# Attention heads taken in pairs: score products of two heads side by side, value products alternating

## The chip, the cores and the metric

The kernel runs on one core of a Trainium2 chip. Its engines are TensorE (PE in the profile, with PEld for its weight loads), VectorE (DVE), ScalarE (ACT), GpSimd (POOL) and SyncE (SP, which issues the transfers). The metric is the device time of one execution in microseconds (us), lower is better; the time before is the median of three runs.

## The reference

Two transformer blocks over 256 tokens of width 1024, all in float32. The first block has two layers; each has 12 self-attention heads and 4 heads over a memory of 256 rows, all of width 64, and a gated feed-forward net. The second block has 8 attention heads of width 96 (values of width 64) beside a recurrent branch, and then a layer of 16384 experts.

```python
# first block, layer 0: forgetting attention (layer 1: causal with ALiBi)
s = q @ k.T * scale + F[t] - F[s]          # causal
out = softmax(s) @ v                       # 12 heads of width 64
mem_out = softmax(qm @ mk.T * scale) @ mv  # 4 heads of width 64, 256 keys
# second block
s = where(mask, q @ k.T * scale, min)      # 8 heads, q and k of width 96
out = softmax(s) @ v                       # v of width 64
```

## The kernel before, in words

Weights stream from DRAM in blocks of 128x1024, 512 KB each. ACT makes a high part `hi` of every block (line L201) and DVE, or for some blocks POOL, the rest `lo` (L203); every projection is then three products per chunk (L238 to L240). A projection of one block is 24 matmuls of 128x256. A block is split two blocks ahead of its use, through three buffers for `lo`.

Attention works with one head at a time. `scores` makes, for the two token tiles, a negated score product on PE (L364); in a self head the first tile has 128 keys and the second 256, in a memory head both have 256. Heads of width 64 use 64 of the array's 128 rows: head 0 of a pair the lower half of the partitions, head 1 the upper half. In layer 0 a second product (L366, 128 rows) adds the forgetting terms at once. DVE adds the mask and takes the row minimum (L369, L373), ACT takes the exponential (L374), DVE scales the rows by their inverse sums (L379, L381): the result is `P`. `values` transposes `P` on PE (L396), copies the transposes to `PT` (ACT at L403 and DVE at L405 in turn), and multiplies by the values (L406, and L408 or L410). Its output has 64 columns of the array: head 0 writes partitions 0 to 63 of a PSUM tile, head 1 partitions 64 to 127. These products have float32 operands, and the trace has two matmuls for each.

`layer` queues the `values` calls: while the scores of pair c are made, the two heads of pair c - 1 wait, and two projections of the next pair's keys and queries lie between. In `mixers` (second block) a head's `values` come after the two `mg` projections of the next head.

The order of instructions on each engine is not that of the code: the framework's scheduler sets it when the program is built, by its own estimate of times. An engine then runs its list in order, and waits on semaphores where a result isn't there.

The tiles that the prediction names: `pa` and `pb` are PSUM tiles (four buffers each), `kT`, `qT`, `mkT`, `qmT`, `QT` keys and queries, `SA` and `MB` the forgetting terms, `V`, `MV`, `KV` values, `xth`/`xtl` and `h1h`/`h1l` the two parts of a projection's input, `hdh`, `at` the heads' output, `rr`, `ii`, `xc` the recurrent branch (scans at L1228, products on POOL at L1227).

Of the kernel before, what the change touches and what calls it, by code (L numbers as in the profile page):

```python
# [8 lines left out]
F32 = mybir.dt.float32  # L9
# [14 lines left out]
#: Buffers of the weight stream, and how many blocks ahead of their use the blocks are split.  # L24
# [16 lines left out]
#: The blocks from which on the row factors of the two norms are there, and the first query block of whole h2.  # L41
# [3 lines left out]
#: The blocks whose low parts gpsimd computes, and the channels that it convolves.  # L45
# [4 lines left out]
#: Expert chunks ahead of the first gates; chunks in the first expert buffer; chunks of the tail.  # L50
# [91 lines left out]
def expert_order():  # L142
    """What the tensor engine does in the expert layer: u chunks, groups of gates, v chunks."""
# [10 lines left out]
class Stream:  # L154
    """Weight blocks from DRAM, each split exactly into two float32r parts (high + low)."""
# [9 lines left out]
    def on_pool(self, key):  # L165
        """Where the vector engine has much else to do, gpsimd takes a part of the subtractions."""
# [52 lines left out]
class Net:  # L219
# [28 lines left out]
    def setup(self):  # L248
# [23 lines left out]
        # the clock of the tensor engine rises with use: have it up when the input arrives  # L272
# [111 lines left out]
    def values(self, state, v, po):  # L384
# [7 lines left out]
        for kb in range(2):  # L392
            for tt in range(2):
                if causal and kb > tt:
                    continue
# [1171 lines left out]
```

## Time and profile before

| what | before |
|---|---|
| time, median of 3 runs | 1764.59 us (1763.13 to 1770.04) |
| profiled execution, first to last instruction | 1766.2 us |
| PE busy in it | 1713.1 us, 97% |
| PEld, DVE, ACT, POOL busy | 1563.5, 1242.2, 888.9, 412.1 us |

The profile records the span of its execution and nothing around it, so 1766.2 us is the profiled execution's own time here; it lies 1.6 us above the median. Matmuls overlap in the pipeline: what one costs is read from the distance between starts, not from its duration. A row of the timeline merges what follows each other: its first number is the start, the second the time from the first start to the last end, and the text names the first of them. A number in square brackets is the idle time ahead of it.

### The profile page before, as it was taken

What the parts mean: (1) busy time and instruction counts of PE and PEld (TensorE: products, weight loads), DVE (VectorE), ACT (ScalarE), POOL (GpSimd) and SP (SyncE); (2) the same over time, 40 slices, a digit from 0 to 9 for tenths busy, and PEclk for the clock granted to TensorE, in tenths of its full rate; (3) what the DMA queues carried; (4) which work ended last, traced back from release to release, by engine and by line L of the source; (5) the groups of instructions that cost most, each with busy time, mean ns of one, the idle gap of its engine ahead of it and who ended that gap; (6) DMA issues with size and microseconds to landing.
All of it is one profiled execution on the core that took longest, in us unless ns stands there. A gap on an engine that the chain in (4) does not pass through costs nothing.

```text
span 1766.2 us, 30939 instructions
## 1 busy us (share of the span) xinstructions
PE 1713.1 (97%) x11722; PEld 1563.5 (89%) x11722; DVE 1242.2 (70%) x2417; ACT 888.9 (50%) x1502; POOL 412.1 (23%) x463
## 2 busy tenths in 40 slices
PE   8999999999999999888999999999999999999998
PEld 7779989888899998777999989999999988888887
DVE  6656767766577768886775968977888755555555
ACT  7444544464454446587654444444444444444443
POOL 5100000001000004344032324278888300000000
PEclk9999999999999999989999999999999999999999
DMA  6324777753377765433456555454444556665663
GB/s 218 119 96 162 251 235 252 255 181 108 111 251 253 254 225 165 137 120 117 158 168 203 172 166 165 156 168 138 138 143 143 179 189 186 189 188 190 190 188 123
DMA packets 86803, 311.44 MB, mean 176 GB/s; under 512 B 9728, under 2 KB 11008, under 8 KB 86144
## 3 DMA queue, kind: packets, MB, share of 16 engines
q1 hardware_dynamic: 86480, 308.43, 53.6%
q8 instruction: 92, 1.51, 0.3%
q10 hardware_dynamic: 144, 1.05, 0.2%
q14 instruction: 55, 0.45, 0.1%
q0 software_dynamic: 32, 0.00, 0.0%
HBM read 307.35 MB, written 2.10 MB: 175 GB/s over the span
## 4 chain that ended last, share of the span: by engine, by line
PE 69%; DVE 16%; DMA 7%; issue 3%; ACT 2%; POOL 1%; SPq 0%; DVEq 0%; ACTq 0%; POOLq 0%
PE pb L240 10%; PE pb L239 10%; PE pa L238 10%; PE pb L238 10%; PE pa L239 10%; PE pa L240 10%; DMA raw<-in_w_ada_dram 6%; DVE lo L203 5%; PE pa L1430 3%; PE pa L364 2%; PE pb L406 1%; ACT hi L201 1%; DMA raw<-in_w_gate_dram 1%; PE pb L396 1%; DVE gu L645 1%
## 5 line engine op out<-in xcount | busy, mean ns | idle before, releaser
L203 DVE TENSOR_TENSOR lo<-raw,hi 128x1024 fp32r<-128x1024 f32 (+3 forms) x498 | 620.5, 1248 | 315.3 <-issue 202.7
L201 ACT ACTIVATE hi<-raw 128x1024 fp32r<-128x1024 f32 (+1 forms) x532 | 555.6, 1046 | 447.3 <-PE pb L239 227.9
L240 PE MATMUL pb<-h1h,lo 128*128 128x256 f32 x1264 | 361.6, 286 | 10.5 <-DVE lo L203 8.9
L238 PE MATMUL pb<-h1h,hi 128*128 128x256 f32 x1264 | 367.4, 291 | 0.8 <-ACT gl L1002 0.8
L239 PE MATMUL pb<-h1l,hi 128*128 128x256 f32 x1264 | 360.8, 285 | 0.0
L240 PE MATMUL pb<-xth,lo 128*128 128x256 f32 (+1 forms) x936 | 266.3, 285 | 3.1 <-DVE lo L203 3.0
L238 PE MATMUL pb<-xth,hi 128*128 128x256 f32 (+1 forms) x936 | 266.1, 285 | 0.0
L239 PE MATMUL pb<-xtl,hi 128*128 128x256 f32 (+1 forms) x936 | 265.3, 284 | 0.0
L240 PEld LDWEIGHTS pb<-h1h,lo 128*128 128x128 f32 x1264 | 242.3, 192 | 13.0 <-DVE lo L203 10.9
L238 PEld LDWEIGHTS pb<-h1h,hi 128*128 128x128 f32 x1264 | 242.5, 192 | 1.7 <-ACT gl L1002 1.0
L239 PEld LDWEIGHTS pb<-h1l,hi 128*128 128x128 f32 x1264 | 242.3, 192 | 0.7 <-issue 0.5
L1429 POOL TENSOR_SCALAR ring<-iota,slots 128x128 f32<-128x128 f32 x256 | 210.2, 835 | 42.4 <-PE pa L1430 42.0
L238 PE MATMUL pa<-hi,ring_v 128*128 128x512 f32 x512 | 202.1, 395 | 0.0
L240 PE MATMUL pa<-hi,ring_v 128*128 128x512 f32 x512 | 202.0, 395 | 0.0
L239 PE MATMUL pa<-lo,ring_v 128*128 128x512 f32 x512 | 202.0, 395 | 0.0
L240 PEld LDWEIGHTS pb<-xth,lo 128*128 128x128 f32 (+1 forms) x936 | 176.9, 189 | 6.4 <-DVE lo L203 4.2
L239 PEld LDWEIGHTS pb<-xtl,hi 128*128 128x128 f32 (+1 forms) x936 | 177.1, 189 | 2.9 <-issue 0.9
L238 PEld LDWEIGHTS pb<-xth,hi 128*128 128x128 f32 (+1 forms) x936 | 176.9, 189 | 2.3 <-issue 0.3
L203 POOL TENSOR_TENSOR lo<-raw,hi 128x1024 fp32r<-128x1024 f32 x34 | 91.4, 2688 | 180.4 <-PE pb L240 117.3
L240 PEld LDWEIGHTS pa<-hi,ring_v 128*128 128x128 f32 x512 | 96.5, 188 | 22.5
L238 PEld LDWEIGHTS pa<-hi,ring_v 128*128 128x128 f32 x512 | 96.5, 188 | 22.5
L239 PEld LDWEIGHTS pa<-lo,ring_v 128*128 128x128 f32 x512 | 96.5, 188 | 22.3
(427 smaller groups left out, 2795.0 us busy)
## 6 DMA issues: line engine op xcount, KB each, us to landing
raw<-in_expert_u_dram SPq DMA_DIRECT2D x128, 512.0 KB, 3.6
raw<-in_expert_v_dram SPq DMA_DIRECT2D x128, 512.0 KB, 4.3
raw<-in_w_ada_dram SPq DMA_DIRECT2D x48, 512.0 KB, 4.5
raw<-in_w_gate_dram SPq DMA_DIRECT2D x44, 512.0 KB, 4.2
raw<-in_w_up_dram SPq DMA_DIRECT2D x44, 512.0 KB, 4.4
raw<-in_w_down_dram SPq DMA_DIRECT2D x44, 512.0 KB, 4.4
raw<-in_w_out_dram SPq DMA_DIRECT2D x24, 512.0 KB, 3.6
raw<-in_w_mg_dram SPq DMA_DIRECT2D x16, 512.0 KB, 3.2
```

Of the source, the lines that this page charges most:

```text
L201: first = nc.scalar.activation(hi[:, :w], raw[:, :w], AF.Copy)
L203: self.last = first, eng.tensor_tensor(lo[:, :w], raw[:, :w], hi[:, :w], OP.subtract)
L238: mm(out, s[0], m[0], start=start, stop=False)
L239: mm(out, s[0], m[1], start=False, stop=False)
L240: mm(out, s[1], m[0], start=False, stop=stop)
L364: nc.tensor.matmul(p[:, :nk], qT[:, ts], kT[:, :nk], start=True, stop=extra is None)
L396: nc.tensor.transpose(pt[:, off:off + 128], P[:, R[tt][0] + kb * 128:R[tt][0] + (kb + 1) * 128], self.ident)
L406: nc.tensor.matmul(po, v(0), PT[:, 0:T], start=True, stop=False, skip_group_check=True)
L645: nc.vector.tensor_tensor(gu, p.rearrange("p (a t) -> p a t", a=2), rb[:, None, :].to_broadcast([128, 2, T]), OP.mult)
L1429: nc.gpsimd.tensor_scalar(ob, iota, slots[:, 1, t:t + 1], None, op0=OP.is_equal)
L1430: nc.tensor.matmul(p[:, j * 128:(j + 1) * 128], oa, ob, start=True, stop=True, skip_group_check=True)
```

## The change

`scores` takes one head or two. With two it makes the products of both heads next to each other (tile 0 of both, then tile 1 of both), all in four PSUM tiles, and only then the four products with the forgetting terms; the exponentials and the scaling follow for both heads. `values` takes a pair: the six (memory: eight) transposes of both heads, a copy of the first head's to `PT` on ACT and of the second's on DVE, then the value products of the two heads in turn, by blocks of 128 keys. In the second block, where q and k have 96 rows, scores are still made for one head at a time, and the values of a pair come together, after the projections that follow its second head. Lines of comment are taken out elsewhere, so line numbers differ.

```diff
-    def scores(self, qT, kT, causal, bias, extra=None):
-        nc = self.nc
-        P, R = self.att.tile([128, 384 if causal else 512], F32, tag="P", name="P"), []
...
+    def scores(self, qk, causal, bias, extra=None):
+
+        nc, n = self.nc, len(qk)
+        ps = []
         for tt in range(2):
             nk = 128 * (tt + 1) if causal else T
             ts = slice(tt * 128, (tt + 1) * 128)
-            p = self.psA()
-            nc.tensor.matmul(p[:, :nk], qT[:, ts], kT[:, :nk], start=True, stop=extra is None)
-            if extra is not None:
-                nc.tensor.matmul(p[:, :nk], extra[0][:, ts], extra[1][:, :nk], start=False, stop=True)
...
+            ps.append([self.psA()[:, :nk] for _ in range(n)])
+            for (qT, kT), p in zip(qk, ps[tt]):
+                nc.tensor.matmul(p, qT[:, ts], kT[:, :nk], start=True, stop=extra is None)
+        if extra is not None:
+            for tt in range(2):
+                for (sel, rows), p in zip(extra, ps[tt]):
+                    nc.tensor.matmul(p, sel[:, tt * 128:(tt + 1) * 128], rows[:, :p.shape[1]], start=False, stop=True)
...
+    def values(self, states, v, po):
+
+        nc = self.nc
+        causal = states[0][1][0][1] == 128
+        PTs = []
+        for s, (P, R) in enumerate(states):
+            pt = self.psB()
+            off = 0
+            for kb in range(2):
+                for tt in range(2):
+                    if causal and kb > tt:
+                        continue
+                    nc.tensor.transpose(pt[:, off:off + 128], P[:, R[tt][0] + kb * 128:R[tt][0] + (kb + 1) * 128],
+                                        self.ident)
+                    off += 128
+            PT = self.att.tile([128, 512], F32, tag="PT", name="PT")
+            if s == 0:
+                nc.scalar.copy(PT[:, :off], pt[:, :off])
             else:
-                s = p
...
+                nc.vector.tensor_copy(PT[:, :off], pt[:, :off])
+            PTs.append(PT)
         for kb in range(2):
...
+            for s, PT in enumerate(PTs):
+                o = po[s * 64:(s + 1) * 64]
+                if kb and causal:
+                    nc.tensor.matmul(o[:, 128:T], v(s, 1), PT[:, T:T + 128], start=False, stop=True,
+                                     skip_group_check=True)
+                else:
+                    nc.tensor.matmul(o, v(s, kb), PT[:, kb * T:(kb + 1) * T], start=kb == 0, stop=kb == 1,
+                                     skip_group_check=True)
...
-            states = []
-            for s in range(2):
-                rows = slice(s * 64, (s + 1) * 64)
-                states.append(self.scores(qmT[rows, b, :], mkT[rows, b, :], False, None))
+            halves = [slice(s * 64, (s + 1) * 64) for s in range(2)]
+            states = self.scores([(qmT[rows, b, :], mkT[rows, b, :]) for rows in halves], False, None)
...
-            finish(1)
-            waiting.append(head_values(h, self.scores(QT[0][:, h, :], QT[1][:, h, :], True, cm)))
+            if h % 2 == 0:
+                finish(0)
+            states += self.scores([(QT[0][:, h, :], QT[1][:, h, :])], True, [cm])
+            if h % 2:
+                waiting.append(pair_values(h - 1, states))
+                states = []
```

The built order of SP and POOL is the same in both programs. That of PE, DVE and ACT differs in three stretches alone: from the first memory scores to the output projection in each of the two layers, and from the `mg` projections to the second block's output projections. Two places show it.

The first is PE in layer 0, between two projections of keys and queries: the scores of one pair (L364, in the changed program L365; `SA` terms at L366, then L369) and the transposes and values of the pair before (L396, L406, L408, then L410, L426, L423). Before:

```order
L364 MATMUL pa<-kT,qT 128x128
L366 MATMUL pa<-MB,SA 128x128
L364 MATMUL pa<-kT,qT 128x256
L366 MATMUL pa<-MB,SA 128x256
L396 MATMUL pb<-ident,P 128x128 x3
L364 MATMUL pa<-kT,qT 128x128
L366 MATMUL pa<-MB,SA 128x128
L364 MATMUL pa<-kT,qT 128x256
L406 MATMUL pb<-PT,V 64x256
L408 MATMUL pb<-PT,V 64x128
L396 MATMUL pb<-ident,P 128x128 x3
```

In the changed program, at the best ordered of the six pairs:

```order
L365 MATMUL pa<-kT,qT 128x256 x2
L369 MATMUL pa<-MB,SA 128x128 x2
L369 MATMUL pa<-MB,SA 128x256 x2
L410 MATMUL pb<-ident,P 128x128 x6
L365 MATMUL pa<-kT,qT 128x128 x2
L365 MATMUL pa<-kT,qT 128x256
L426 MATMUL pb<-PT,V 64x256 x2
L423 MATMUL pb<-PT,V 64x128 x2
```

The products with 64 rows, with 128 rows and with 64 columns, which took turns one by one, now stand in groups. In the other pairs the scheduler has put some of them elsewhere: one score product of a pair alone, or two to nine projection matmuls between the first value product of head 0 and that of head 1. The memory scores stand as four in a row in both programs.

The second place is the first pair of the second block, on PE: before, the transposes of its first head (`P_8754`), the scores of two later heads, the first head's values, and then 48 projection matmuls ahead of the second head's transposes.

```order
L396 MATMUL pb_8929<-ident_94,P_8754 128x128 x3
L364 MATMUL pa_8940<-QT1_8260,QT0_8259 128x128
L364 MATMUL pa_8945<-QT1_8260,QT0_8259 128x256
L364 MATMUL pa_9037<-QT1_8260,QT0_8259 128x128
L364 MATMUL pa_9042<-QT1_8260,QT0_8259 128x256
L406 MATMUL pb_8928<-PT_8933,KV_8230 64x256
L408 MATMUL pb_8928<-PT_8933,KV_8230 64x128
```

In the changed program the second head's transposes (`P_8845`) follow at once, the values of both heads stand together, and the 48 matmuls come behind them, with 48 more ahead of the next pair's transposes:

```order
L410 MATMUL pb_8929<-ident_94,P_8758 128x128 x3
L410 MATMUL pb_8935<-ident_94,P_8845 128x128 x3
L365 MATMUL pa_8947<-QT1_8260,QT0_8259 128x128
L365 MATMUL pa_8949<-QT1_8260,QT0_8259 128x256
L365 MATMUL pa_9034<-QT1_8260,QT0_8259 128x128
L365 MATMUL pa_9036<-QT1_8260,QT0_8259 128x256
L426 MATMUL pb_8928<-PT_8933,KV_8230 64x256
L426 MATMUL pb_8928<-PT_8939,KV_8230 64x256
L423 MATMUL pb_8928<-PT_8933,KV_8230 64x128
L423 MATMUL pb_8928<-PT_8939,KV_8230 64x128
```

DVE at the same place, in the changed program: the scans of the recurrence, the scaling of the second head's `P_8845`, the `lo` parts of two weight blocks, and then the copy `PT_8939` that the second head's values need. Before, the same rows stand there without the copy.

```order
L1237 SCALAR_TENSOR_TENSOR rr_8257<-rr_8257,ii_8258 128x256 x4
L393 RECIPROCAL inv_8854<-sums_8846 128x2
L395 TENSOR_SCALAR P_8845<-P_8845,inv_8854 128x128
L395 TENSOR_SCALAR P_8845<-P_8845,inv_8854 128x256
L203 TENSOR_TENSOR lo_8897<-raw_8726,hi_8896 128x1024
L203 TENSOR_TENSOR lo_8971<-raw_8781,hi_8970 128x1024
L417 COPY PT_8939<-pb_8935 128x384
```

So PE reaches the need for `P_8845` and `PT_8939` 48 matmuls sooner, while DVE's list ahead of them is as long as before.

## Rows read from the trace of the kernel before

**Rows 1.** The page: its span and the busy time of the engines.
```profile
span 1766.2 us, 30939 instructions
PE 1713.1 (97%) x11722; PEld 1563.5 (89%) x11722; DVE 1242.2 (70%) x2417; ACT 888.9 (50%) x1502; POOL 412.1 (23%) x463
```

**Rows 2.** Busy time by stretch: layer 0, layer 1, second block.
```profile
core 0: us, PE busy (x) PEld busy (x) DVE busy (x) ACT busy (x) POOL busy (x), PEclk, DMA share, GB/s
50.00:144.00 94.00, 91.94 (x601) 75.12 (x602) 54.02 (x153) 40.53 (x99) 0.00 (x0) 0.98 0.29 96
394.00:476.00 82.00, 81.55 (x580) 67.53 (x577) 52.17 (x151) 39.88 (x97) 8.54 (x10) 1.00 0.31 102
776.00:856.00 80.00, 73.79 (x532) 68.34 (x533) 51.79 (x104) 62.94 (x116) 28.12 (x27) 0.92 0.34 119
```

**Rows 3.** PE's longest waits in layer 0 (first row) and in layer 1.
```profile
PE pa L364 <- DVE qmT L588: 1.7, 1, 1.7
...
PE pb L406 <- ACT PT L403: 0.2, 1, 0.2
```

**Rows 4.** Timeline of PE, layer 0: scores and values of one pair.
```profile
101.14 0.48 PE L364 MATMUL pa<-kT,qT 64*128 64x128 f32 x2
101.55 0.33 PE L366 MATMUL pa<-MB,SA 128*128 128x128 f32 x1
101.81 0.70 PE L364 MATMUL pa<-kT,qT 64*128 64x256 f32 x2
102.44 0.39 PE L366 MATMUL pa<-MB,SA 128*128 128x256 f32 x1
102.67 0.49 PE L396 MATMUL pb<-ident,P 128*128 128x128 f32 x3
...
104.39 0.65 PE L406 MATMUL pb<-PT,V 128*64 128x256 f32 x2
104.87 0.38 PE L408 MATMUL pb<-PT,V 128*64 128x128 f32 x2
105.18 0.55 PE L396 MATMUL pb<-ident,P 128*128 128x128 f32 x3
```

**Rows 5.** Timeline of PE, layer 0: projections, memory scores of one pair, projection.
```profile
53.40 0.28 PE L238 MATMUL pb<-xth,hi 128*128 128x256 f32 x1
53.52 0.28 PE L239 MATMUL pb<-xtl,hi 128*128 128x256 f32 x1
53.73 1.14 PE L364 MATMUL pa<-mkT,qmT 64*128 64x256 f32 x8
54.80 0.38 PE L240 MATMUL pb<-xth,lo 128*128 128x256 f32 x1
```

**Rows 6.** Timeline of PE, layer 1: scores of two heads in a row, of one head.
```profile
409.95 0.93 PE L364 MATMUL pa<-kT,qT 64*128 64x128 f32 x8
...
413.16 0.92 PE L364 MATMUL pa<-kT,qT 64*128 64x128 f32 x4
414.01 0.65 PE L406 MATMUL pb<-PT,MV 128*64 128x256 f32 x2
```

**Rows 7.** Timeline of PE, second block: scores, then values of two heads.
```profile
798.11 1.48 PE L364 MATMUL pa<-QT,QT 96*128 96x128 f32 x8
800.07 0.65 PE L406 MATMUL pb<-PT,KV 128*64 128x256 f32 x2 [0.48 <-ACT PT L403]
...
813.59 1.11 PE L406 MATMUL pb<-PT,KV 128*64 128x256 f32 x2 [5.61 <-DVE PT L405]
```

**Rows 8.** Timeline of DVE over the same stretch.
```profile
800.20 1.27 DVE L381 TENSOR_SCALAR P<-P,inv 128x128 f32<-128x128 f32 x2
801.40 3.44 DVE L203 TENSOR_TENSOR lo<-raw,hi 128x1024 fp32r<-128x1024 f32 x2
...
813.00 0.53 DVE L405 COPY PT<-pb 128x384 f32<-128x384 f32 x1
```

**Rows 9.** Busy time and granted clock behind the long wait (columns as in group 2).
```profile
813.60:818.90 5.30, 5.30 (x22) 4.58 (x23) 0.81 (x3) 2.94 (x4) 0.00 (x0) 0.50 0.35 137
```

More of the change, by code (lines that the diff above doesn't have):

```diff
@@ L374, in scores @@
-            nc.scalar.activation(P[:, off:off + nk], s[:, :nk], AF.Exp, bias=mn[:, tt:tt + 1], scale=-1.0,
-                                 accum_out=sums[:, tt:tt + 1])
-            R.append((off, nk))
-            off += nk
-        inv = self.small.tile([128, 2], F32, tag="inv", name="inv")
-        nc.vector.reciprocal(inv, sums)
-        for tt, (off, nk) in enumerate(R):
-            nc.vector.tensor_scalar(P[:, off:off + nk], P[:, off:off + nk], inv[:, tt:tt + 1], None, op0=OP.mult)
-        return P, R
@@ new lines, in scores @@
+            for (qT, kT), p in zip(qk, ps[tt]):
[4 more added lines that the diff above has]
+                    nc.tensor.matmul(p, sel[:, tt * 128:(tt + 1) * 128], rows[:, :p.shape[1]], start=False, stop=True)
+        got = []
+        for k in range(n):
+            P = self.att.tile([128, 384 if causal else 512], F32, tag="P", name="P")
+            sums = self.small.tile([128, 2], F32, tag="sums", name="sums")
+            mn = self.small.tile([128, 2], F32, tag="mn", name="mn")
+            R, off = [], 0
+            for tt in range(2):
+                p = ps[tt][k]
+                nk = p.shape[1]
+                if bias is not None:
+                    s = self.att.tile([128, T], F32, tag="s", name="s")
+                    nc.vector.tensor_tensor_reduce(out=s[:, :nk], in0=p, in1=bias[k][:, T - nk:], scale=1.0,
+                                                   scalar=0.0, op0=OP.add, op1=OP.min, accum_out=mn[:, tt:tt + 1])
+                else:
+                    s = p
+                    nc.vector.tensor_reduce(mn[:, tt:tt + 1], p, axis=AX.X, op=OP.min)
+                nc.scalar.activation(P[:, off:off + nk], s[:, :nk], AF.Exp, bias=mn[:, tt:tt + 1], scale=-1.0,
+                                     accum_out=sums[:, tt:tt + 1])
+                R.append((off, nk))
+                off += nk
+            got.append((P, R, sums))
@@ L571, in pair_values, with go @@
         def pair_values(states, v, chunk):
-            po = [None]
-            def one(s):
-                def go():
-                    if s == 0:
-                        po[0] = self.psB()
-                    self.values(states[s], lambda kb: v(s, kb), po[0][s * 64:(s + 1) * 64, :T])
-                    if s == 1:
-                        self.split(self.xT_chunk(heads, chunk), po[0][:, :T])
-                return go
-            waiting.extend([one(0), one(1)])
+            def go():
+                po = self.psB()[:, :T]
+                self.values(states, v, po)
+                self.split(self.xT_chunk(heads, chunk), po)
+            waiting.append(go)
         for b in range(2):
@@ L610, in layer @@
                 keys_queries(c + 1)
-            finish(2)
-            states = []
-            for s in range(2):
-                hd = 2 * c + s
-                rows = slice(s * 64, (s + 1) * 64)
-                if i == 0:
-                    bias, extra = self.causal, (self.SA[:, hd, :], self.MB)
-                else:
-                    bias = self.att.tile([128, T], F32, tag="alibi", name="alibi", bufs=2)
-                    nc.gpsimd.tensor_scalar(bias, self.dist, 2.0 ** (-8.0 * (hd + 1) / 12), None, op0=OP.mult)
-                    extra = None
-                states.append(self.scores(qT[rows, c, :], kT[rows, c, :], True, bias, extra))
+            finish(1)
+            bias, extra = [self.causal] * 2, None
+            if i == 0:
+                extra = [(self.SA[:, 2 * c + s, :], self.MB) for s in range(2)]
+            else:
+                bias = []
+                for s in range(2):
+                    bias.append(self.att.tile([128, T], F32, tag="alibi", name="alibi", bufs=2))
+                    nc.gpsimd.tensor_scalar(bias[s], self.dist, 2.0 ** (-8.0 * (2 * c + s + 1) / 12), None, op0=OP.mult)
+            halves = [slice(s * 64, (s + 1) * 64) for s in range(2)]
+            states = self.scores([(qT[rows, c, :], kT[rows, c, :]) for rows in halves], True, bias, extra)
             pair_values(states, lambda s, kb, c=c: V[:, kb, (2 * c + s) * 64:(2 * c + s + 1) * 64], c)
-            finish(2)
+            finish(1)
         xt2, los = self.new_xt(), []
@@ L1122, in mixers @@
         waiting = []
-        po = [None]
         def finish(n):
```

53 lines of the change are left out of this document (13 added, 40 removed).

## The prediction

> **What bounds the kernel now.** I read the page first: PE is busy for 1713.1 of 1766.2 us [rows 1], so a change counts by what it does to PE's list, or to the few waits in it. Then the windows over the three stretches where the built orders differ [rows 2]: in layer 0 PE is busy for 91.94 of 94 us and in layer 1 for 81.55 of 82 us, both near full clock, while DVE and ACT have a third or more of the time free, and the longest waits are 1.7 us ahead of the first memory scores and 0.2 us [rows 3]. There a microsecond less on PE's list is a microsecond less in the end. The third stretch, in the second block, is different: PE is busy for 73.79 of 80 us at a mean clock of 0.92 [rows 2]; it waited 5.61 us for a copy on DVE [rows 7], and behind that wait it ran at half clock for some 5.3 us [rows 9]. Everything outside these stretches has the same order on all engines and keeps its time.
>
> **What a product costs.** The timeline gives starts, and I price by their distances. Between projections it is 0.12 us (53.40 to 53.52 [rows 5]). A float32 score product against 256 keys alone among 128-row products took 0.63 us (101.81 to 102.44), one against 128 keys 0.41 us (101.14 to 101.55) [rows 4]. With u for streaming 128 columns once and s for going into the 64-row form and out of it, 4u + s = 0.63 and 2u + s = 0.41, so u = 0.11 and s = 0.19. The memory scores of two heads, four products of 256 keys in a row, took 1.07 us (53.73 to 54.80 [rows 5]): 8u + 0.19, and not 16u. So two heads in different row halves already run at the same time when they stand together. Layer 1 says the same: eight matmuls of two heads lasted 0.93 us, four of one head 0.92 us [rows 6]. The value products of one head took 0.48 + 0.31 = 0.79 us (104.39 to 105.18 [rows 4]), which is 6u + 0.13. Going back to 128 rows shows in the forgetting products, 0.26 and 0.23 us (101.55 to 101.81, 102.44 to 102.67 [rows 4]): against 0.11 and 0.12 of streaming this is 0.11 to 0.15 more. I take 0.15 us for each change of form, the mean of 0.19, 0.13 and 0.13.
>
> **The sum on PE.** I counted both built orders.
> Changes of form: 77 to 49 in layer 0, 50 to 46 in layer 1, 16 to 10 in the second block. 38 fewer at 0.15 us are 5.7 us; the bounds 0.13 and 0.19 give 4.9 and 7.2.
> Score streaming: in layer 0 the self scores stood alone, 12 heads of 6u = 72u; side by side wherever the scheduler left a pair together, 52u. In layer 1 without the forgetting products several pairs were together already: 62u to 48u. The memory scores stay. 34u are 3.7 us. The second block's scores have 96 rows and gain nothing.
> Value streaming, if two heads in different column halves also run at the same time: 104u to 80u in each layer (the scheduler has parted many pairs by projections), 48u to 28u in the second block; 68u are 7.5 us. No row of before shows two column halves next to each other, so the bounds are 0 and 7.5. I take 7.5, by the nearest row, the row halves of [rows 5, 6].
> Together 16.9 us less; the forgetting products, transposes and projections keep their number.
>
> The Trainium skill, page "TensorE: Matmul & The Clock Gate", section on packing small matmuls, gives 2.38x for three column tiles and no figure for two float32 ones; no run here shows it. Scaled to two tiles that would be 1.59x, an estimate by that page: 136u of paired streaming would shrink by 50u and not by 68u, and the sum would be 14.9 us.
>
> **The waits.** In the second block the second head's transposes follow the first's at once. Before, PE was through the first's at 798.11 [rows 7], but `P_8845` is scaled on DVE only at 800.20 + 1.27 = 801.47 [rows 8], behind the scans: PE will wait 3.4 us there. Then transposes (0.32) and eight score matmuls (1.48 [rows 7]) take it to 803.3, the first head's 256-key product to 803.75. The second's copy stands on DVE behind two `lo` parts that end at 801.40 + 3.44 = 804.84, and takes 0.53 us more [rows 8]: 805.4, a wait of 1.6 us. These 5.0 us replace the old waits of 0.48 and 5.61 us [rows 7]: the copy that PE waited for at 813.59 came 48 matmuls too soon behind its transposes, and now 96 matmuls (96 x 0.12 = 11.5 us) give DVE time for its scans and `lo` parts first. So 1.1 us less. I take the half clock as it is, since 5.0 us of waiting are still there; if it doesn't fall, 5.3 / 2 = 2.7 us come on top [rows 9].
> In the two layers the scheduler sets both copies behind the transposes with some score products as cover, about 1 us, and the second copy stands on DVE behind the four mask operations of the pair. Of the time for a copy (0.53 [rows 8]) I take a fifth as uncovered: 0.1 us for each of 16 pairs, 1.6 us; the bounds are 0 and all of it, 8.5 us. A projection's eviction or a `lo` part behind these copies has the next block's 24 x 0.12 = 2.9 us as cover.
>
> Sum: 1766.2 - 16.9 - 1.1 + 1.6 = 1749.8 us against the profiled execution. That one lies 1.6 us above the median of the runs, so I forecast a median of 1748 us, 0.9% faster. The bounds of the terms give 1742 to 1763 if all fall on one side.
>
> **Rivals.**
> A. The value products don't overlap: 7.5 us less gain, 1755.5 us. For it: no row shows column halves together. Against: row halves do overlap, and the program places the two heads in separate halves of the columns.
> B. The copies are uncovered in the layers: PE waits 0.5 us in all 16 pairs, 6.9 us more than taken, 1755 us. For it: four transposes or three per head used to be followed by more products ahead of the first use. Against: waits were 0.2 us at the same places before [rows 3].
> C. Slower, by one mechanism: in the second block PE waits at each of the four pairs as it did at 813.59, because DVE, whose list is paced by the scans and by `lo` parts that took 3.44 / 2 = 1.7 us each [rows 8], is never ahead of the transposes that now come sooner. Four waits of 5.61 us with 2.7 us of half clock are 33 us, in place of the 8.3 us of one old wait with its half clock and the 0.5 us of the other: 1766.2 - 16.9 + 1.6 + 33 - 8.8 - 1.6 = 1773 us. It takes over from about three such waits (3 x 8.3 = 24.9 us, past the gain of 15.3 us and the 8.8 us given back). For it: the first pair does wait, by the rows. Against: 96 and 48 matmuls stand ahead of the later pairs, and the scans end by then.
> D. The change does nothing for scores, since two heads are together already: true of the memory scores and of the one pair of [rows 6], but 12 heads of layer 0 stood alone [rows 4].
> E. The clock doesn't fall in the second block, or the waits there vanish: 1741 to 1745 us.
>
> **How the numbers follow.** Chances: forecast 50%, A 18%, B 12%, C 7%, D 2%, E 11%. No change within 0.5% (8.8 us, about what a measurement of this kernel can tell, the three runs before being 7 us apart) means above 1755.8 us. A and B straddle that bound, half each. Faster: 50 + 11 + 9 + 3, less what the forecast's own spread loses, 0.70; within 0.5%: 0.23; slower: 0.07. The range reaches over A, B and E: 1740 to 1759 us.
>
> **What the changed profile would show.** Step 1, fewer changes of form: rows of `x4` forgetting products at some 0.12 us each. Step 2: scores of two heads starting together, so that eight matmuls last about 0.93 us in layer 0 too. Step 3: value products of two heads in a row taking about 6u + 0.13 = 0.8 us for the pair; 1.5 us would mean A. Step 4: in the second block a wait of about 3.4 us ahead of transposes from `P` and about 1.6 us ahead of value products from `PT` on DVE, none of 5.6 us, and the stretch some 4 us shorter; layer 0 about 9 us and layer 1 about 4.5 us shorter. New waits for `PT` of over 0.3 us per pair in the layers would make the forecast wrong on the slow side.

## The result and the profile after

The changed kernel takes 1750.59 us (median of 4 runs, 1749.45 to 1754.1) against 1765.36 us for the kernel before on the same chip: a ratio of 0.991, 95% interval 0.9889 to 0.993. Timed again later beside three other versions it took 1748.13 us against 1768.16 us, 0.989 (0.987 to 0.991). The forecast was 1748 us, 0.9% faster.

The page's span and busy line of the changed kernel, which answer to [rows 1]:

```profile
span 1751.6 us, 30941 instructions
PE 1700.0 (97%) x11722; PEld 1555.4 (89%) x11722; DVE 1240.8 (71%) x2417; ACT 886.6 (51%) x1501; POOL 411.1 (23%) x463
```

Busy time by stretch in the changed kernel, columns as in [rows 2], with each window's ends moved, to within 0.4 us, to the places of PE's program at which the windows of [rows 2] begin and end:

```profile
50.00:134.40 84.40, 81.96 (x605) 68.92 (x604) 54.98 (x153) 40.90 (x100) 0.00 (x0) 1.00 0.32 107
382.60:459.80 77.20, 77.00 (x578) 64.51 (x575) 52.33 (x151) 39.70 (x97) 8.71 (x10) 1.00 0.33 110
763.30:838.00 74.70, 71.17 (x532) 66.48 (x533) 51.85 (x104) 61.11 (x115) 28.97 (x27) 0.93 0.37 127
```

The same work takes 84.40, 77.20 and 74.70 us in place of 94, 82 and 80: 9.6, 4.8 and 5.3 us less, 19.7 in all. The whole span is only 14.6 us shorter, so 5.1 us came back in code that is the same in both programs. The table further down shows that this is the spread of executions.

One pair of layer 0 on PE's timeline, the one whose order stands in the second fence of the change; it answers to [rows 4]:

```profile
95.93 0.70 PE L365 MATMUL pa<-kT,qT 64*128 64x256 f32 x4
96.56 0.73 PE L369 MATMUL pa<-MB,SA 128*128 128x128 f32 x4
97.14 0.82 PE L410 MATMUL pb<-ident,P 128*128 128x128 f32 x6
97.88 1.23 PE L365 MATMUL pa<-kT,qT 64*128 64x128 f32 x6
99.04 0.83 PE L426 MATMUL pb<-PT,V 128*64 128x256 f32 x4
99.52 0.57 PE L423 MATMUL pb<-PT,V 128*64 128x128 f32 x4
```

Four forgetting products take 97.14 - 96.56 = 0.58 us from start to start; in [rows 4] two of them took 0.49 us. The value products of both heads for the first block of keys take 0.48 us (99.04 to 99.52), as long as those of one head in [rows 4] (104.39 to 104.87). The whole pair takes 0.98 us from its first start to the next product, where one head took 0.79 us. The longest waits, as totals, times and the longest, in layer 0 (first row, answers to [rows 3]) and around the second block's first pair:

```profile
PE pa L365 <- DVE qmT L599: 1.7, 1, 1.7
...
PE pb L410 <- DVE P L395: 3.0, 2, 2.6
```

The lists of the two layers have no wait for a copy `PT`; the idle gaps at value products are 0.14 us at most. The second block's first pair, PE's timeline (answers to [rows 7]):

```profile
787.85 0.30 PE L410 MATMUL pb<-ident,P 128*128 128x128 f32 x1 [2.59 <-DVE P L395]
788.51 0.69 PE L410 MATMUL pb<-ident,P 128*128 128x128 f32 x2 [0.36 <-DVE P L395]
788.99 2.77 PE L365 MATMUL pa<-QT,QT 96*128 96x128 f32 x8
791.69 1.31 PE L426 MATMUL pb<-PT,KV 128*64 128x256 f32 x3
```

and DVE's (answers to [rows 8]):

```profile
783.80 3.31 DVE L1237 TENSOR_TENSOR_SCAN rr<-rr,ii 128x256 f32<-128x256 f32 x3
...
787.19 1.26 DVE L395 TENSOR_SCALAR P<-P,inv 128x128 f32<-128x128 f32 x2
788.38 3.42 DVE L203 TENSOR_TENSOR lo<-raw,hi 128x1024 fp32r<-128x1024 f32 x2
791.72 0.55 DVE L417 COPY PT<-pb 128x384 f32<-128x384 f32 x1
```

The second head's `P` is scaled behind the scans, and PE waits 2.59 + 0.36 us for it, where 3.4 was forecast. Then PE's clock is at the lower level, 1.2 GHz (columns as above; granted 0.50 of full):

```profile
788.99:794.10 5.11, 5.11 (x18) 3.42 (x18) 4.03 (x9) 0.61 (x2) 4.33 (x5) 0.50 0.49 174
```

The eight score matmuls take 2.77 us in place of the 1.48 of [rows 7], and so the copy `PT`, done at 791.72 + 0.55 = 792.27 us, is no longer waited for.

### The profile page after: what moved, and what is told of

Read it like the earlier page. It is cut to its first block, busy times and chain, and to the rows that moved or that the text cites. A ratio compares the mean times of both kernels' runs of the same rounds, so it can differ in the third digit from the quotient of the medians.

```text
span 1751.6 us, 30941 instructions
## 1 busy us (share of the span) xinstructions
PE 1700.0 (97%) x11722; PEld 1555.4 (89%) x11722; DVE 1240.8 (71%) x2417; ACT 886.6 (51%) x1501; POOL 411.1 (23%) x463
## 3 DMA queue, kind: packets, MB, share of 16 engines
q10 hardware_dynamic: 144, 1.05, 0.1%
## 4 chain that ended last, share of the span: by engine, by line
PE 66%; DVE 17%; DMA 10%; issue 4%; ACT 2%; POOL 1%; SPq 0%; DVEq 0%; ACTq 0%; POOLq 0%
PE pa L238 10%; PE pa L239 10%; PE pa L240 10%; PE pb L240 10%; PE pb L238 9%; PE pb L239 9%; DMA raw<-in_w_ada_dram 8%; DVE lo L203 6%; PE pa L1439 3%; PE pa L365 1%; PE pb L426 1%; DVE gu L653 1%; ACT hi L201 1%; DVE raw L725 1%; PE pb L410 1%
```

## The experiments

The stretches in the expectations run from the first memory score to the first product of `lo` with `hdh` (layers), and from the first `QT` product to the first product with `rth` (second block). In the layers the last values still alternate with the output projection behind that end. So the table also has the whole layer, to the 81st product of the output projection, and in the column "rest" what is left of the time to PE's last matmul. All are differences of starts in the traces, in us; the ratio is that to the kernel before in the same comparison, with its interval.

| run | layer 0 | layer 1 | second block | whole layer 0 | whole layer 1 | rest | median | ratio |
|---|---|---|---|---|---|---|---|---|
| before | 77.57 | 66.13 | 72.27 | 92.31 | 80.90 | 1515.8 | 1765.36 | 1 |
| changed | 68.35 | 62.03 | 67.95 | 82.17 | 76.20 | 1520.4 | 1750.59 | 0.991 (0.9889 to 0.993) |
| e1 scores apart | 74.05 | 63.87 | 67.49 | 87.96 | 77.93 | 1520.3 | 1760.67 | 0.9946 (0.9927 to 0.9965) |
| e2 values apart | 71.82 | 65.01 | 71.19 | 86.52 | 79.78 | 1517.8 | 1761.96 | 0.9954 (0.9934 to 0.9973) |
| e3 in turn | 67.22 | 62.58 | 67.44 | 80.81 | 77.53 | 1519.4 | 1750.0 | 0.9882 (0.9847 to 0.9916) |
| e4 second block before | 68.28 | 62.03 | 72.45 | 82.10 | 76.20 | 1522.8 | 1751.97 | 0.9893 (0.9859 to 0.9927) |
| e5 before again | 75.95 | 66.13 | 72.36 | 90.69 | 80.89 | 1517.9 | 1768.5, one run | |
| e6 changed again | 68.20 | 62.03 | 65.40 | 81.94 | 76.19 | 1518.4 | 1748.13 | 0.989 (0.987 to 0.991) |
| e7 values later | 68.35 | 62.02 | 73.96 | 82.09 | 76.19 | 1519.5 | 1757.89 | 0.9938 (0.9919 to 0.9957) |
| e8 together | 67.16 | 60.10 | 75.18 | 80.09 | 73.11 | 1521.0 | 1753.54 | 0.9907 (0.989 to 0.9925) |
| e9 products later | 61.73 | 56.44 | 67.86 | 74.66 | 69.71 | 1520.7 | 1737.18 | 0.9816 (0.98 to 0.9832) |
| e10 scans behind | 68.22 | 62.03 | 65.86 | 82.04 | 76.20 | 1516.8 | 1747.0 | 0.9877 (0.9859 to 0.9895) |
| e11 combined | 61.59 | 56.45 | 64.06 | 74.53 | 69.73 | 1517.4 | 1732.58 | 0.9808 (0.9786 to 0.9829) |

A stretch repeats within 0.2 us from one execution to the next where its clock is the same (layer 1: 62.02 or 62.03 in all five executions that share its order), while the rest scatters over 7 us. So the stretches tell versions apart better than the medians do.

The second block is the least steady of the three, and its differences are good to about 1 us. Its end comes before or behind the last value products: of their 32 matmuls it holds 28 in the kernel before, e2, e4 and e5, 26 in e7, e8 and e11, and 32 in the others (four of them, one head's, take 0.8 us). And its first projections run in part at a low clock, for a time that differs: from the first score product to the next, with 48 projections between, it took 7.64 us in e5, 7.30 us in the changed kernel and 6.06 us in e6.

**e1, scores apart.** The scores are made for one head at a time, each forgetting product behind its score product; values as changed.

```diff
-            for (qT, kT), p in zip(qk, ps[tt]):
+            for k, ((qT, kT), p) in enumerate(zip(qk, ps[tt])):
                 nc.tensor.matmul(p, qT[:, ts], kT[:, :nk], start=True, stop=extra is None)
-        if extra is not None:
-            for tt in range(2):
...
+                if extra is not None:
+                    nc.tensor.matmul(p, extra[k][0][:, ts], extra[k][1][:, :nk], start=False, stop=True)
...
-            states = self.scores([(qT[rows, c, :], kT[rows, c, :]) for rows in halves], True, bias, extra)
+            states = [self.scores([(qT[rows, c, :], kT[rows, c, :])], True, bias[s:s + 1], extra and extra[s:s + 1])[0]
+                      for s, rows in enumerate(halves)]
```

> The changed kernel with the scores of one head at a time, each forgetting product straight behind its score product; values still in pairs. Stretches are from the first memory score to the first product of lo with hdh (layers) and from the first QT product to the first product with rth (second block); the changed kernel has 68.35, 62.03 and 67.95 us, the kernel before 77.57, 66.13 and 72.27 us. My theory (26 more changes of form at 0.15 us and 20 more units of 0.11 us in layer 0, 16 more units in layer 1): layer 0 about 74.4 us, layer 1 about 63.8 us, second block as it was; the whole about 8 us more than the changed kernel, 0.995 of the kernel before. Rival, that score products side by side give nothing beyond fewer changes of form: layer 0 about 72.2 us, layer 1 unchanged at 62.0 us. Rival, that the values do it all: no stretch moves.

Measured: 74.05, 63.87 and 67.49 us, within 0.5 us of the theory in all three. The scores side by side are worth 5.7 us in layer 0 and 1.8 us in layer 1. Layer 1 has as many changes of form in both versions, so its gain is streaming at the same time alone: 1.84 / 16 = 0.115 us a unit. With that price, layer 0's 26 changes are left with (5.7 - 20 x 0.115) / 26 = 0.13 us each.

**e2, values apart.** Transposes, copy and products of head 0, then those of head 1.

```diff
-            PTs.append(PT)
-        for kb in range(2):
-            for s, PT in enumerate(PTs):
-                o = po[s * 64:(s + 1) * 64]
+            o = po[s * 64:(s + 1) * 64]
+            for kb in range(2):
```

> The changed kernel with the values of one head behind the other (transposes, copy and products of head 0, then of head 1); scores still in pairs. My theory (value products of two column halves overlap): layer 0 about 72.2 us in place of 68.35, layer 1 about 65.7 in place of 62.03, second block about 71 in place of 67.95; the whole some 10 us over the changed kernel, 0.997 of the kernel before. Rival (column halves don't overlap, and the scores' order gives the rest): layer 0 at most 1.2 us more (8 changes of form), layer 1 at most 0.6 us more, second block 0.9 us more.

Measured: 71.82, 65.01 and 71.19 us, within 0.7 us of the theory. The rival (at most 1.2 and 0.6 us in the layers) falls: value products in pairs are worth 3.5 us in layer 0 and 3.0 us in layer 1. Of this 0.7 and 0.5 us are new short waits of PE; what is left, 2.8 and 2.5 us, is still far over the rival's value. In the second block PE now waits 3.3 us for the copy on DVE.

**e3, in turn.** Transposes and copies of both heads as changed, but all products of head 0 ahead of those of head 1.

```diff
-        for kb in range(2):
-            for s, PT in enumerate(PTs):
+        for s, PT in enumerate(PTs):
+            for kb in range(2):
```

> The changed kernel with both heads' transposes and copies as they are, but the value products of head 0 ahead of those of head 1 in place of alternating. The built order parts fewer pairs by projections in layer 0 (40 changes of form in place of 49). Theory I, that what overlaps is whatever stands in the same run of 64-column products, in any order: layer 0 about 65.5 us (68.35 less 2.9), layer 1 about 62.4, second block about 67.3; the whole 3 us less than the changed kernel. Theory II, that products of two column halves overlap only where they alternate: layer 0 about 69.2, layer 1 about 65.0, second block about 69.9; the whole 5 to 6 us more than the changed kernel.

Measured: 62.58 and 67.44 us in layer 1 and the second block, Theory I to 0.2 us; layer 0 at 67.22 lies between the two. By the whole layer, layer 1 lies between them too: 77.53 - 76.20 = 1.3 us over the changed kernel, where Theory I has 0.4 and Theory II 3.0 us. PE's timeline shows one pair of layer 0 in this version:

```profile
108.55 0.83 PE L426 MATMUL pb<-PT,V 128*64 128x256 f32 x4
109.03 0.57 PE L423 MATMUL pb<-PT,V 128*64 128x128 f32 x4
```

The list there has head 0's 256-key product, its 128-key product, then head 1's. In time all four 256-key matmuls come first: head 1's ran beside head 0's, although two of head 0's stand ahead of it in the list. So the alternation is not what makes the products overlap. In layer 0 the eight value matmuls of one memory pair took 1.60 us to the start of what follows, those of the other 1.05 us. At the first of these pairs the second copy ended 0.54 us behind the start of head 0's products, and the heads overlapped little; at the other both copies were done. The same 1.60 us with the same late copy stands in layer 1. Both theories left out when the second operand is there; e8 and e9 try that.

**e4, the second block as before.** `mixers` has its old loop (one head's `values` after the next head's `mg` projections); both layers as changed.

```diff
-            if h % 2 == 0:
-                finish(0)
-            states += self.scores([(QT[0][:, h, :], QT[1][:, h, :])], True, [cm])
-            if h % 2:
-                waiting.append(pair_values(h - 1, states))
-                states = []
+            finish(1)
+            waiting.append(head_values(h, self.scores([(QT[0][:, h, :], QT[1][:, h, :])], True, [cm])))
```

> The changed kernel with the second block as it was before (values of one head at a time, one block later); both layers have the changed kernel's order. My theory: layers as in the changed kernel (68.35 and 62.03 us), second block back at about 72.3 us with its wait of 5.6 us for the copy on DVE and the half clock behind it; the whole about 4.3 us over the changed kernel. Rival, that the second block's gain was an accident of one execution: its stretch within 1.5 us of 67.95 us, with shorter waits than before.

Measured: 72.45 us with the wait of 5.6 us for `PT` back, and the layers to 0.1 us those of the changed kernel. The parts of the change add up, and the second block's gain belongs to its own edit. The median alone (1751.97 us) would not have told this.

**e5 and e6, both kernels once more, unchanged.**

> The kernel before once more, for a second trace. Outside the three stretches the kernels share one order on every engine; there the first trace of before had 1545.1 us, that of the changed kernel 1548.4 us and the four experiments so far 1547.2 to 1550.8 us. If the 3 us are the spread of executions: this trace has about 1548 us outside, stretches of 77.6, 66.1 and 72.3 us within 0.5 us. If the change itself costs 3 us outside: about 1545 us again.

> The changed kernel once more, beside the two that follow. Stretches 68.35, 62.03 and 67.95 us within 0.5 us, outside 1547 to 1551 us; 0.990 to 0.992 of the kernel before.

Two things come out. The rest was 1517.9 and 1518.4 us, against 1515.8 and 1520.4 in the first pair of traces: the 5.1 us that "came back" (4.6 us by the table, whose stretches end elsewhere) are spread, not a price of the change. And layer 0 of before took 75.95 us, not 77.57: in the first trace PE was at half clock behind the 1.7 us wait of [rows 3]. Busy time and clock, columns as above, first in the first trace of before, then in that of e5:

```profile
54.00:64.00 10.00, 8.28 (x57) 7.41 (x56) 8.05 (x23) 7.14 (x19) 0.00 (x0) 0.85 0.53 188
```

```profile
54.00:64.00 10.00, 8.40 (x67) 7.40 (x66) 8.41 (x24) 7.47 (x20) 0.00 (x0) 1.00 0.57 197
```

In e6 the second block took 65.40 us. Its waits and the clock behind them:

```profile
PE pb L410 <- DVE P L395: 3.0, 2, 2.6
PE pb L426 <- DVE PT L417: 1.5, 1, 1.5
```

```profile
785.00:797.00 12.00, 7.56 (x54) 6.00 (x53) 10.91 (x20) 7.76 (x14) 8.62 (x9) 1.00 0.27 89
```

The same program, the same 3.0 us wait, and this time no fall of the clock; the wait of 1.5 us for `PT`, forecast as 1.6, now shows.

The 67.95 - 65.40 = 2.55 us between the two traces are not all the clock behind this wait, though. From the first score product of the stretch to the next, ahead of the wait, the first trace of the changed kernel took 1.24 us longer, at a lower clock (columns as above, first trace, then e6):

```profile
764.93:772.23 7.30, 7.30 (x52) 7.30 (x52) 2.86 (x7) 5.24 (x13) 1.23 (x2) 0.79 0.44 154
```

```profile
766.44:772.50 6.06, 6.06 (x51) 6.06 (x51) 2.16 (x5) 5.05 (x12) 1.23 (x2) 0.97 0.46 174
```

So 1.3 us are left for what follows, and they are a net figure: the half clock cost about 2.8 us there and hid the wait of 1.5 us.

**e7, the second block's values one block later.**

```diff
-            if h % 2 == 0:
+            if h % 2:
                 finish(0)
```

> The changed kernel with one edit: in the second block a pair's values come one block (48 matmuls) later, ahead of the next pair's second scores. PE's list has the same matmuls and as many changes of form. My theory (the wait of 2.6 + 0.4 us for P behind the scans, and some 3.5 us lost at half clock behind it, come from transposes that are due too soon): second block 67.95 - 3.0 - 3.5 = about 61.5 us, and the whole 6 us less than the changed kernel, 0.987 of the kernel before. Rival (DVE is simply full there, so the wait moves to a later copy or scaling): second block 66 to 68 us, a wait of some 3 us at another line. Rival for the clock alone: the wait goes and half clock stays, about 65 us.

Measured: 73.96 us, 6 to 8.6 us more than the changed kernel. My theory fell, and the rival was too mild. PE:

```profile
794.69 0.82 PE L410 MATMUL pb<-ident,P 128*128 128x128 f32 x6
...
798.85 0.65 PE L426 MATMUL pb<-PT,KV 128*64 128x256 f32 x2 [2.46 <-ACT PT L415]
803.24 0.69 PE L426 MATMUL pb<-PT,KV 128*64 128x256 f32 x1 [3.75 <-DVE PT L417]
```

ACT and DVE over the same time:

```profile
795.04 1.28 ACT L386 ACT_TABLE_LOAD   x1
...
797.09 1.05 ACT L201 ACTIVATE hi<-raw 128x1024 fp32r<-128x1024 f32 x1
...
798.30 0.49 ACT L415 COPY PT<-pb 128x384 f32<-128x384 f32 x1
```

```profile
795.86 6.01 DVE L1237 TENSOR_TENSOR_SCAN rr<-rr,ii 128x256 f32<-128x256 f32 x4 [1.11 <-POOL ii L1236]
...
802.63 0.55 DVE L417 COPY PT<-pb 128x384 f32<-128x384 f32 x1
```

`P` was ready, but the transposes now fall just ahead of the second group of scans on DVE and behind a table load and a `hi` part on ACT, and each copy waits for its place in that engine's list. Elsewhere in the stretch PE waited 2.0 us for `P`, 1.5 us for a `lo` part and 0.6 us for `at`. What a wait costs hangs on what stands ahead of the releaser in its list, and later is not the same as better.

**e8, pairs kept together.** The edit of e7, and in the layers an order-only edge that sets head 0's first value product behind the second head's copy; in layer 0 both copies on ACT.

```diff
-            if s == 0:
-                nc.scalar.copy(PT[:, :off], pt[:, :off])
+            if s == 0 or self.on_act:
+                last = nc.scalar.copy(PT[:, :off], pt[:, :off])
...
+                    if s == 0 and kb == 0:
+                        self.tc.add_manual_dep(mm.ins, last.ins.name, mybir.DependencyInfo(
+                            mybir.DependencyClass.NoSync, mybir.DependencyReason.DATA), reason="pair")
```

> The edit of e7, and the pairs kept together in the layers: an order-only edge sets the first value product of head 0 behind the second head's copy, and in layer 0 ACT makes both copies. In the built order changes of form go from 49 to 32 in layer 0 and from 46 to 30 in layer 1; score streaming in paired units from 68 to 56 and from 64 to 56, value streaming from 80 to 52 and from 80 to 60. My theory (0.15 us a change, 0.11 us a unit, no new waits): layer 0 about 61.4 us in place of 68.35, layer 1 about 56.5 in place of 62.03, second block as in e7; the whole some 19 us under the changed kernel, 0.980 of the kernel before. Rival (the projections that parted the pairs hid the copies, so PE now waits about 0.5 us at each of 16 pairs): layer 0 about 65 us, layer 1 about 60 us, with rows of waits for PT.

Measured: 67.16 and 60.10 us in the layers, 2.2 us over the rival's value in layer 0, at it in layer 1. My theory fell, by 5.8 and 3.6 us. The rows of waits that the rival named are hardly there, 1.2 us in layer 0 and none in the list of layer 1, so most of the loss has another form. One pair of layer 0, PE and then ACT:

```profile
89.45 0.65 PE L426 MATMUL pb<-PT,V 128*64 128x256 f32 x2
90.34 0.43 PE L426 MATMUL pb<-PT,V 128*64 128x256 f32 x1 [0.24 <-ACT PT L415]
```

```profile
88.09 0.46 ACT L415 COPY PT<-pb 128x384 f32<-128x384 f32 x1
...
89.83 0.46 ACT L415 COPY PT<-pb 128x384 f32<-128x384 f32 x1
```

Three exponentials stand between the two copies on ACT. Head 0's products run alone, then PE waits 0.24 us: the pair is together in the list and apart in time. In layer 1 four pairs took 1.46 to 1.47 us each, with a second copy that ended 0.61 to 0.62 us behind their start. The projections that parted the pairs in the changed kernel had hidden that copy.

**e9, products one block later in the layers.** `values` is cut in two: transposes and copies stay where they are, the products come 48 matmuls later. The second block is the changed kernel's.

```diff
-                self.values(states, v, po)
-                self.split(self.xT_chunk(heads, chunk), po)
+                PTs = self.transposes(states)
+
+                def end():
+                    po = self.psB()[:, :T]
+                    self.products(states, PTs, v, po)
+                    self.split(self.xT_chunk(heads, chunk), po)
+                ends.append(end)
...
         def finish(n):
+            while ends:
+                ends.pop(0)()
```

> The changed kernel with the values of the layers in two steps: transposes and copies where they are, the value products one block (48 matmuls, 5.7 us) later, ahead of the next pair's scores. In the built order every pair stands together: changes of form go from 49 to 32 in layer 0 and from 46 to 29 in layer 1, paired score streaming from 68 to 56 and 64 to 56 units, value streaming from 80 to 60 and 80 to 56; the second block is the changed kernel's. Theory I, that what e8 fell short by in the layers (67.2 and 60.1 us in place of 61.4 and 56.5) was the second head's copy, so that head 0's products ran alone: the copies now have 5.7 us, and layer 0 takes about 62.3 us, layer 1 about 56.0 us; the whole 12 us less than the changed kernel, 0.983 of the kernel before. Theory II, that the price of 0.11 us a unit and 0.15 us a change is too high: layer 0 at least 65.5 us, layer 1 at least 59.5 us.

Measured: 61.73 and 56.44 us, within 0.6 us of Theory I. PE at one pair of layer 0:

```profile
90.91 0.65 PE L432 MATMUL pb<-PT,V 128*64 128x256 f32 x4
91.39 0.39 PE L429 MATMUL pb<-PT,V 128*64 128x128 f32 x4
91.71 0.93 PE L365 MATMUL pa<-kT,qT 64*128 64x128 f32 x8
92.57 0.73 PE L369 MATMUL pa<-MB,SA 128*128 128x128 f32 x4
93.13 0.82 PE L410 MATMUL pb<-ident,P 128*128 128x128 f32 x6
```

The value products of both heads take 91.71 - 90.91 = 0.80 us, the 0.79 us that one head took in [rows 4], and the scores of both heads 0.86 us. This is the pair as the prediction priced it. Against the expectation not every pair is like that: the built order still parts two of the eight pairs in layer 0 and one in layer 1, as the counts of 60 and 56 units say (52 would be all), and two more of layer 1 had a late second copy.

The traces show how the lateness counts. Over the pairs whose eight value matmuls stand in one run, take the time from its start to what follows, and the end of the second copy from the same start. Self pairs: copy ahead 0.80 us (e9), 0.13 us late 0.98 us (the changed kernel, where the heads alternate, and e3, where they go in turn), 0.36 us late 1.21 us (e3), 0.62 us late 1.47 us (e8). Memory pairs: copy ahead 1.02 us (e9), 0.54 us late 1.60 us (e3 and e9), 0.74 us late 1.80 us (the changed kernel). The last of these, PE (the next product starts at 405.60 us) and then DVE, and the one in e9 with the copy ahead (the next product starts at 402.35 us):

```profile
403.80 1.87 PE L426 MATMUL pb<-PT,MV 128*64 128x256 f32 x8
```

```profile
403.87 0.67 DVE L417 COPY PT<-pb 128x512 f32<-128x512 f32 x1
```

```profile
401.33 1.08 PE L432 MATMUL pb<-PT,MV 128*64 128x256 f32 x8
```

The run grows by about as much as the copy is late, whatever the order in the run. The second block of e9 has the changed kernel's order, but its 67.86 us agree with 67.95 by chance: the wait for `P` was 4.3 us, and its first projections ran at a higher clock.

**e10, scans behind the second head's `P`.**

```diff
-        self.recurrence(rr, ii)
+        with self.tc.issue_after(first.ins):
+            self.recurrence(rr, ii)
```

Here `first` is the scaling of the second head's `P`.

> The changed kernel with an order-only edge on DVE: the scans of the recurrence come behind the scaling of the second head's P. PE's order in the second block is unchanged. If the wait for P comes from the scans ahead of it on DVE's list: the 2.6 + 0.4 us for P go, but two scans and two lo parts (2.3 + 3.4 us) still stand ahead of the copy, which then ends near 6 us behind the transposes; PE waits about 3 us for PT on DVE in place of 1.5. Second block about 64 us with a full clock (65.4 before), 66 to 67 with half clock behind the wait (67.95 before). Rival (P is late for its exponentials on ACT, not for the scans): a wait for P of over 2 us stays. Rival (the waits just go with the edge): second block at 61 us.

Measured: 65.86 us, at a mean clock of 0.72 between 788 and 794 us. PE's waits around the pair:

```profile
PE pb L427 <- DVE PT L418: 2.1, 1, 2.1
PE pb L427 <- ACT PT L416: 0.7, 2, 0.5
```

The wait for `P` is gone, so the scans had caused it; most of it is now the wait for `PT` behind two `lo` parts, as expected, if shorter (2.1 us, 3 expected). What the edge gave in time isn't shown: the low clock behind the wait is milder than in the changed kernel's first trace (0.50 over 5.11 us there), and 65.86 us lie between its two traces, 67.95 and 65.40 us.

**e11, combined.** e9 and e10, and both copies of the second block on ACT (`self.on_act`, as in e8, set in `mixers`).

> The edits of e9 and e10 together, and in the second block both copies on ACT, where the second stands right behind the first and not behind lo parts. Layers as in e9 (62.3 and 56.0 us). Second block: without the waits for P (3.0 us) and PT (1.5 us) and with a full clock about 61 us; ACT's later exponentials and table loads change places, and as in e7 that can raise a new wait: 64 to 70 us then. The whole about 1732 us, 0.979 of the kernel before, if both hold; 1736 to 1742 us with a new wait.

Measured: 1732.58 us, 0.9808 (0.9786 to 0.9829), with layers as in e9. The second block is at 64.06 us: the waits for `P` and `PT` are down to 0.2 us, and a new one of 2.4 us, for the minimum of a later head's scores on DVE, takes part of it back. Both e9 and e11 beat the changed kernel, which had 0.989 (0.987 to 0.991); between the two the intervals overlap.

## Why the prediction was right, point by point

**PE's list, 16.9 us less.** Right in place and size. By the table the whole layers gave 90.69 - 81.94 = 8.75 us and 80.89 - 76.19 = 4.70 us (both at full clock), where the counts of the prediction give 9.0 us for layer 0 (28 changes, 20u and 24u) and 4.8 us for layer 1 (4 changes, 14u and 24u), before the copies. The second block's share (6 changes and 20u, 3.1 us) isn't shown by itself. e1 and e2 take the two halves apart and find the scores and the values each at their price; e9, with 17 fewer changes of form and 32 fewer units in each layer (17 x 0.15 + 32 x 0.11 = 6.1 us), gains 81.94 - 74.66 = 7.3 us and 76.19 - 69.71 = 6.5 us more.

**Column halves run at the same time (7.5 us, from 0 to 7.5).** The upper bound was the true one. Rival A falls by e2 and by the 0.80 us of a pair in e9. The prediction took the overlap from the list alone; the runs add the condition that the second copy is there, and in the changed kernel itself a pair in one run took 0.98 and 1.80 us, not 0.80 and 1.02. The estimate by the Trainium skill, page "TensorE: Matmul & The Clock Gate", section on packing small matmuls (1.59x for two tiles), is lower than what the trace has here: two heads in the time of one, 0.80 against 0.79 us.

**The second block's waits (1.1 us less).** The two waits came at the places that were computed: 2.6 + 0.4 us for `P` (forecast 3.4) and, in e6, 1.5 us for `PT` (forecast 1.6). In the first trace the clock fell behind the first wait, PE came later to the second, and it vanished. So that trace had 3.0 us of waits, not the 5.0 of the sum, and yet its stretch was 72.27 - 67.95 = 4.3 us shorter, as the terms had it (0.9 + 2.2 + 1.1 = 4.2): that agreement is in part luck, and no run takes it apart. The half clock was taken as staying; it stayed in the first trace and was gone in e6. Rival E priced that at 2.7 us; net of the wait for `PT` that came with it, it was worth 1.3 us.

**Copies in the layers (1.6 us more).** The size is near, the mechanism was another. The term stood for PE waiting 0.1 us at each of 16 pairs, and no such wait is in the lists. Seven of the eight pairs in each layer are parted by other matmuls, which covered the copy at a price that the count already held. The one pair of each layer that stands in one run had a late second copy, and its heads ran partly apart: 0.98 - 0.80 and 1.80 - 1.02, 1.0 us together. As a row of waits Rival B is false for the changed kernel; in e8, where the cover is taken away, layer 1 has its size, and both layers have few of its waits.

**Rival C.** PE does wait at the first pair, but not at the other three, as the sum said. e7 shows that the mechanism is real: with the transposes at another place the waits for `P` and `PT` came to 8.3 us (2.5 and 3.8 us at one pair, 2.0 us at another).

**What was read wrongly.** The clock of 0.98 for layer 0 in [rows 2] was passed over as near full. It was a stretch at half clock, worth 77.57 - 75.95 = 1.6 us, in that one execution. It made the first pair of traces show a gain in layer 0 that is 1.6 us too large. The forecast's sum didn't rest on it. In the chances, half of A and half of B are 9 and 6; the 3 that was added for B is a quarter, which moves the chance of faster by 0.03.

In all the three stretches lost 245.48 - 226.32 = 19.2 us in the first pair of traces and 243.94 - 223.53 = 20.4 us in the second, where 16.4 was forecast. The layers at full clock gave 8.75 + 4.70 = 13.5 us, for 9.0 + 4.8 - 1.6 = 12.2 forecast; the rest of the excess is the clock, of layer 0 in the first trace of before, and of the second block in the second pair. That the first median fell 2.6 us from the forecast and the second 0.1 us is closer than the case allows: code that no edit touched, the column "rest", differs by 7 us between the traces.

## What to carry to other kernels

Products in different halves of the array overlapped here when they stood in one run of the list and the operands of both were there; their order inside the run didn't matter. So put the products a block behind the copies that feed them (e9), and don't only tie them together (e8). A wait costs what stands ahead of its releaser in that engine's list: look at that list at the new place before moving the consumer, for a later place can be worse (e7).

## What the runs showed of the hardware that was not expected

**Matmuls of different column halves don't keep the order of the list.** In e3 head 1's 256-key matmuls, the first of them at 108.74 us, started before head 0's 128-key matmuls, the first at 109.03 us, which stand ahead of them in PE's list. What is said ahead of the prediction, that an engine runs its list in order, has this exception.

**The clock behind the same wait differs between executions.** After PE had idled for 2.6 and 0.4 us the granted clock was 0.50 in one execution of the changed kernel and 1.00 in the other.

**Scans take longer beside POOL.** In e6 four scans took 4.44 us, 1.1 us each, while POOL was at work all the time; three scans of the next group, with POOL idle from 794.05 to 799.50 us, took 1.85 us together, 0.6 us each. DVE and then POOL:

```profile
782.95 4.44 DVE L1237 TENSOR_TENSOR_SCAN rr<-rr,ii 128x256 f32<-128x256 f32 x4
...
794.25 1.85 DVE L1237 TENSOR_TENSOR_SCAN rr<-rr,ii 128x256 f32<-128x256 f32 x3
```

```profile
782.00 3.76 POOL L1236 TENSOR_TENSOR ii<-ii,xc 128x256 f32<-128x256 f32 x4
785.73 3.60 POOL L1163 TENSOR_TENSOR rr<-rr,gl 128x256 f32<-128x256 f32 x4
789.76 4.29 POOL L1236 TENSOR_TENSOR ii<-ii,xc 128x256 f32<-128x256 f32 x4 [0.43 <-ACT xc L1234]
799.50 2.39 POOL L203 TENSOR_TENSOR lo<-raw,hi 128x1024 fp32r<-128x1024 f32 x1 [5.45 <-DVE inv L393]
```

Likewise a `lo` part took 1.22 us on DVE in layer 0, where POOL is idle, and 3.42 / 2 = 1.7 us in the second block. The Trainium skill, page "Advanced Engine Details and Errata", section on GPSIMD details, says that POOL shares a read and a write interface with DVE and conflicts with its instructions that have two SBUF inputs; these rows agree. No run takes POOL's products away from the same scans, so the cause is argued from what stands beside what. In e10 one scan of 0.66 us overlaps a POOL product for three quarters of its time by the profile, whose POOL spans are rough, and is not longer.
